# Depthwise convolution split between TensorE and VectorE: 13 taps as full diagonal matmuls against 16 taps as 32x32 diagonal blocks

## The chip, the cores and the metric

One core of a Trainium2 chip runs the whole program in one launch. The metric is device time in microseconds (us), the median of three runs. A profile of one execution goes with it; its times count from its first instruction.

## What is computed

The reference is a stack of four transformer layers on 256 positions of 1024 channels: a convolution mixer with a dense feed-forward layer, a windowed attention layer with a mixture of eight experts, and two hybrid attention layers. The change touches only the depthwise convolution of the first mixer:

```
u = a * sigmoid(gate)                                # 256 positions x 768 channels
u_pad = pad(u, 30 zero positions in front)
c[s, ch] = sum over tap 0..30 of dw_w[tap, ch] * u_pad[s + tap, ch] + dw_b[ch]
c = silu(layer_norm(c))                              # mean and variance over the 768 channels
m = memory_attention(q_mem, mem_k, mem_v)
h = h + concat(c, m) @ w_out
```

## The kernel before

Activations lie with channels on the 128 partitions and the 256 positions along the row. The 768 channels of the convolution are six blocks `t` of 128 channels; `U[t]` (line 1063) holds one block with 30 zeros in front, so a tap is a slice `U[t][:, tap:tap + 256]`. In TensorE terms the weights of a matmul are its stationary operand and the slice is its moving one.

`conv_layer` (line 1057) first projects the input: a loop over `c` = 0, 1, 2 makes two channel blocks at a time from a value half and a gate half, with weights that are split in two fp32r parts (ScalarE writes the high part, VectorE the low part) and three matmuls for each product. VectorE scales the result, ScalarE takes the sigmoid, VectorE writes `U[t]`. Then the 31 taps of a block are shared out. VectorE does the first 18: one `tensor_scalar` and 17 `scalar_tensor_tensor` into `cv[c]` (lines 1099 to 1104). TensorE does the last `PE_TAPS` = 13 in `taps(t)` (line 1067): for each tap ScalarE makes a 128x128 diagonal matrix from the identity (line 1076), and a full fp32 matmul multiplies it with the slice of `U[t]`, all into half of one PSUM bank. After two blocks one VectorE instruction adds that bank to `cv[c]` (line 1081). The profile shows an fp32 matmul as two records.

After the taps come the layer norm (lines 1128 to 1156: a mean by matmul with a constant matrix, subtraction, squares, variance, a reciprocal root on VectorE, a broadcast by matmul, silu, and the split in two fp32r parts), the queries and keys of the memory attention (`mem_first`, line 1017, has sixteen fp32 matmuls 512 columns wide), the memory attention itself, and the output projection `residual` (line 1044) into `xT`. Its first six of eight feed blocks come from the convolution, the last two from the attention. The feed-forward layer needs `xT`.

The order of the instructions is not that of the code. Every operation is recorded with its buffers (`Recorder`), and `issue` (line 555) plays the engines forward in time with prices from `cost` (line 391): each engine takes the first operation in order of priority that is ready and gets its buffers. Priority is the place in the code in TensorE time plus a bias in ns; a negative bias (`TAP_BIAS`, line 38, for the taps on both engines) pulls an operation forward. All operations are issued from line 699, so in the profile they share that line, and go by the kinds of their buffers: `large` (28 buffers for weights, also the diagonal matrices), `gen` (38 buffers for activations), `bank` (the 8 PSUM banks), `ct` and `pt` (constants and parameters). A PSUM bank that is held by one tile is free for another only when its last reader has run; so the eight banks are shared by the projections, the taps, `mem_first` and the layer norm. All DMAs are issued in order from SyncE's queue. `stream` (line 464) is the order's model of TensorE's clock.

Of the kernel before, what the change touches and what calls it, by code (L numbers as in the profile page):

```python
# [11 lines left out]
F32 = mybir.dt.float32  # L12
# [3 lines left out]
OP = mybir.AluOpType  # L16
# [20 lines left out]
PE_TAPS = 13  # L37
TAP_BIAS = -5e3
# [70 lines left out]

def _pairs_cols():  # L110
    return np.concatenate([np.arange(h * HD, (h + 1) * HD) for p in SWA_PAIRS for h in p])
# [5 lines left out]
def _params(i):  # L117
# [5 lines left out]
        ("dw_w", i["cv_dw_w"][0].reshape(CW, 6, 128).transpose(2, 1, 0).reshape(128, 6 * CW)),  # L123
# [25 lines left out]
def _consts():  # L149
# [26 lines left out]
    def add(n, a):  # L176
        nonlocal at
        a = np.ascontiguousarray(a, dtype=f)
        cols[n] = (at, a.shape[1])
        out.append(a)  # L180
        at += a.shape[1]

    add("ident", np.eye(128))
    add("ones", np.ones((128, 128)))
# [158 lines left out]
class Recorder:  # L343
# [47 lines left out]
    def cost(eng, name, outs, ins, kw):  # L391
# [8 lines left out]
        if eng == "PE":  # L400
            w = n(outs[0])
            if name == "transpose":
                w *= 2
            elif ins[0].dtype == F32R:
                w = max(256, w) * 16 / 15 + 4
            else:
                w = 4 * max(w, n(ins[0])) + 6
                if outs[0].ap[0][1] == 32:
                    w /= 4
            return (w + 6) / 2.4, 0.0  # L410
# [9 lines left out]
    def add(self, eng, name, fn, args, kw):  # L420
# [9 lines left out]
        op.work = (op.dur * 2.4, ins[0].ap[0][1] / 128) if eng == "PE" else None  # L430
# [271 lines left out]
class Net:  # L702
# [354 lines left out]
    def conv_layer(self):  # L1057
# [9 lines left out]
        def taps(t):  # L1067
            nc.bias = TAP_BIAS
            dt = [nc.tile("raw", [128, 8, 128]) for _ in range(2)]
            c = cv[t // 2][:, t % 2]  # L1070
            if t % 2 == 0:
                self.pd = self.mm("pcv")
            pd = self.pd[:, t % 2 * S:t % 2 * S + S]
            for n, tap in enumerate(range(CW - PE_TAPS, CW)):
                dg = dt[n // 8][:, n % 8]
                nc.scalar.activation(dg, self.C("ident"), AF.Copy, scale=self.P("dw_w", t * CW + tap))
                nc.tensor.matmul(pd, dg, U[t][:, tap:tap + S], start=n == 0 and t % 2 == 0,
                                 stop=n == PE_TAPS - 1, skip_group_check=True)
            if t % 2:
                c = cv[t // 2]  # L1080
                nc.vector.tensor_tensor(c, c, self.pd.rearrange("p (a s) -> p a s", a=2), op=OP.add)
            nc.bias = 0
# [623 lines left out]
```

## Time and profile before

| | |
|---|---|
| median of three runs | 2171.06 us (2170.19 to 2176.07) |
| the profiled execution | 2170.37 us, of which the profile's span is 2168.5 us |
| TensorE busy in the span | 2129.9 us, granted clock 0.993 of full speed |
| VectorE and ScalarE busy | 976.4 us and 739.3 us |
| the convolution layer | from 0 to about 130 us of the span |

TensorE is busy nearly throughout, so the question for any change is what its own work costs, and whether another engine makes it wait. A matmul's record also holds its latency, so a row's mean is longer than the pace at which matmuls follow one another: the pace is read from how many start in a stretch that is full.

### The profile page before, as it was taken

What the parts mean: (1) busy time and instruction counts of PE and PEld (TensorE: products, weight loads), DVE (VectorE), ACT (ScalarE), POOL (GpSimd) and SP (SyncE); (2) the same over time, 40 slices, a digit from 0 to 9 for tenths busy, and PEclk for the clock granted to TensorE, in tenths of its full rate; (3) what the DMA queues carried; (4) which work ended last, traced back from release to release, by engine and by line L of the source; (5) the groups of instructions that cost most, each with busy time, mean ns of one, the idle gap of its engine ahead of it and who ended that gap; (6) DMA issues with size and microseconds to landing.
All of it is one profiled execution on the core that took longest, in us unless ns stands there. A gap on an engine that the chain in (4) does not pass through costs nothing. (4 is left out here: it accounts for less than half of the span.)

```text
span 2168.5 us, 57713 instructions
## 1 busy us (share of the span) xinstructions
PE 2129.9 (98%) x25554; PEld 1684.8 (78%) x25554; DVE 976.4 (45%) x2085; ACT 739.3 (34%) x1318; POOL 0.2 (0%) x4
## 2 busy tenths in 40 slices
PE   8999999999999999999999999999999999999998
PEld 8799998766565566656565655788999998899997
DVE  8985569530211102020211120666675566667553
ACT  8574447510100001010101010645554454555442
POOL 0000000000000000000000000000000000000000
PEclk9999999999999999999999999999999999999998
DMA  7445554489999999999999997753456555345550
GB/s 260 158 146 191 176 191 159 163 306 407 379 345 406 373 407 342 384 384 405 368 364 378 401 374 285 256 191 113 154 190 194 183 182 188 113 137 194 194 183 29
DMA packets 155633, 555.70 MB, mean 256 GB/s; under 512 B 17392, under 2 KB 20080, under 8 KB 155376
## 3 DMA queue, kind: packets, MB, share of 16 engines
q1 hardware_dynamic: 155376, 551.94, 70.0%
q8 instruction: 202, 3.31, 0.6%
q14 instruction: 55, 0.45, 0.1%
HBM read 550.82 MB, written 1.05 MB: 254 GB/s over the span
## 5 line engine op out<-in xcount | busy, mean ns | idle before, releaser
L699 PE MATMUL bank<-large,gen 128*32 128x256 f32 (+2 forms) x16528 | 1049.3, 379 | 2.7 <-PEq L1330 2.7
L699 PE MATMUL bank<-gen,large 128*128 128x256 f32 x7488 | 934.8, 285 | 9.8 <-ACT large L699 8.1
L699 PEld LDWEIGHTS bank<-large,gen 128*32 128x32 f32 (+1 forms) x16528 | 648.8, 114 | 368.0 <-issue 11.0
L699 PEld LDWEIGHTS bank<-gen,large 128*128 128x128 f32 x7488 | 908.9, 189 | 25.9 <-issue 9.9
L699 DVE TENSOR_TENSOR large<-large,large 128x1024 fp32r<-128x1024 f32 (+1 forms) x364 | 438.5, 1210 | 134.1 <-PE bank L699 91.0
L699 ACT ACTIVATE large<-large 128x1024 fp32r<-128x1024 f32 (+1 forms) x364 | 373.5, 1045 | 241.6 <-PE bank L699 108.2
L699 ACT ACTIVATE gen<-bank 32x256 fp32r<-32x256 f32 (+6 forms) x315 | 121.2, 395 | 917.1 <-PE bank L699 905.8
L699 DVE SCALAR_TENSOR_TENSOR gen<-bank,small,gen 128x256 f32<-128x256 f32 (+2 forms) x100 | 44.3, 446 | 681.3 <-ACT gen L699 681.3
L699 ACT ACTIVATE gen<-gen 128x512 f32<-128x512 f32 (+3 forms) x145 | 86.9, 611 | 156.7 <-DVE gen L699 155.5
L699 DVE TENSOR_TENSOR gen<-bank,gen 32x256 fp32r<-32x256 f32 (+2 forms) x166 | 83.1, 508 | 125.3 <-PE bank L699 65.1
L699 PE MATMUL bank<-gen,gen 128*128 128x192 f32 (+5 forms) x668 | 108.7, 343 | 9.4 <-ACT gen L699 6.0
L699 DVE TENSOR_TENSOR gen<-gen,gen 128x512 f32<-128x512 f32 (+3 forms) x126 | 79.2, 636 | 53.0 <-ACT gen L699 51.3
L699 PEld LDWEIGHTS bank<-gen,gen 64*128 64x128 f32 (+3 forms) x668 | 67.8, 176 | 45.0 <-DVE gen L699 15.8
L699 PE MATMUL bank<-ct,gen 128*128 128x128 f32 (+2 forms) x366 | 62.8, 276 | 8.0 <-DVE gen L699 8.0
L699 PEld LDWEIGHTS bank<-ct,gen 128*128 128x128 f32 (+1 forms) x366 | 44.1, 156 | 24.4 <-issue 12.3
L699 DVE TENSOR_TENSOR xT<-xT,bank 128x512 f32<-128x512 f32 x64 | 43.5, 686 | 24.4 <-PE bank L699 23.5
L699 ACT ACTIVATE gen<-bank,small 128x256 f32<-128x256 f32 (+2 forms) x75 | 41.0, 569 | 31.1 <-PE bank L699 23.6
L699 DVE SCALAR_TENSOR_TENSOR gen<-bank,gen 128x256 f32<-128x256 f32 (+1 forms) x66 | 25.4, 428 | 54.7 <-PE bank L699 54.2
L699 DVE SCALAR_TENSOR_TENSOR gen<-gen,pt,gen 128x256 f32<-128x256 f32 (+1 forms) x120 | 49.0, 485 | 1.7 <-ACT gen L699 1.7
L699 ACT ACTIVATE gen<-gen,small 128x128 f32<-128x128 f32 x72 | 31.8, 443 | 17.8 <-DVE small L699 17.8
L699 PE MATMUL bank<-large,large 128*32 128x256 f32 (+1 forms) x416 | 37.6, 373 | 0.0
L699 DVE STREAM_TRANSPOSE gen<-gen 128x256 f32<-128x256 f32 (+1 forms) x90 | 36.0, 406 | 2.6
(62 smaller groups left out, 412.7 us busy)
## 6 DMA issues: line engine op xcount, KB each, us to landing
large<-e_in SPq DMA_DIRECT2D x448, 512.0 KB, 7.1
large<-e_down SPq DMA_DIRECT2D x224, 512.0 KB, 7.4
large<-c_up SPq DMA_DIRECT2D x64, 512.0 KB, 4.5
large<-c_dn SPq DMA_DIRECT2D x64, 512.0 KB, 4.7
large<-c_g SPq DMA_DIRECT2D x48, 512.0 KB, 3.8
large<-c_qk SPq DMA_DIRECT2D x24, 512.0 KB, 4.8
large<-cv_gate SPq DMA_DIRECT2D x22, 512.0 KB, 4.8
large<-cv_up SPq DMA_DIRECT2D x22, 512.0 KB, 5.6
```

What stands on the lines that cost most here:

```text
L699: op.fn(*[real(x) for x in op.args], **{k: real(x) for k, x in op.kw.items()})
```

## The change

`PE_TAPS` goes from 13 to 16, so VectorE keeps 15 taps of a block. The diagonal matrices of ScalarE go; a block's 16 diagonals are made as 32x32 diagonal blocks by one VectorE instruction, `dg` of 128 partitions x 16 x 32. A tap then is four matmuls of 32 rows by 32 columns, each on its own 32 rows of the array. So that sixteen such matmuls touch sixteen different places of the array, taps are dealt out by `_turn`: tap turn `n` puts its row group `r` on the output partitions of group `(r + n) % 4`. For that SyncE issues six DMAs for each block that write three copies of `U[t]` turned by 32, 64 and 96 partitions, and the four matmuls read the copy that fits; all 64 matmuls of a block wait for all six. The four turns add up in four PSUM banks, where one was used, and four VectorE adds bring them into `cv[c]`. The parameters of the taps are turned on the host in the same way. `TAP_BIAS` goes from -5e3 to -20e3, and the order's prices get an entry for a matmul of 32x32, a full fp32 matmul's divided by 5.2.

```diff
-PE_TAPS = 13
-TAP_BIAS = -5e3
+PE_TAPS = 16
+TAP_BIAS = -20e3
...
+def _turn(n):
+    return (n - CW + PE_TAPS) % 4 if n >= CW - PE_TAPS else 0
+
+
+def _turned(w):
+
+    return np.stack([np.roll(w[:, :, n], -32 * _turn(n), axis=0) for n in range(w.shape[2])], 2)
...
-        ("dw_w", i["cv_dw_w"][0].reshape(CW, 6, 128).transpose(2, 1, 0).reshape(128, 6 * CW)),
+        ("dw_w", _turned(i["cv_dw_w"][0].reshape(CW, 6, 128).transpose(2, 1, 0)).reshape(128, 6 * CW)),
...
+    add("ident4", np.tile(np.eye(32), (4, 1)))
...
                 if outs[0].ap[0][1] == 32:
-                    w /= 4
+                    w /= 4 if ins[0].ap[0][1] > 32 else 5.2
...
-        op.work = (op.dur * 2.4, ins[0].ap[0][1] / 128) if eng == "PE" else None
+        op.work = (op.dur * 2.4, max(32, ins[0].ap[0][1]) / 128) if eng == "PE" else None
+        if op.work and ins[0].ap[0][1] == 32:
+            op.work = op.dur * 2.4, 1
...
         def taps(t):
             nc.bias = TAP_BIAS
-            dt = [nc.tile("raw", [128, 8, 128]) for _ in range(2)]
-            c = cv[t // 2][:, t % 2]
+            turned = nc.tile("raw", [128, 3, CW - 1 + S])
+            moves = []
+            nc.bias = -2 * LOAD_FIRST
+            for n in range(1, 4):
+                at = 128 - 32 * n
+                nc.sync.dma_start(turned[:at, n - 1], U[t][32 * n:])
+                moves.append(nc.ops[-1])
+                nc.sync.dma_start(turned[at:, n - 1], U[t][:32 * n])
+                moves.append(nc.ops[-1])
+            nc.bias = TAP_BIAS
+            dg = []
+            all16 = [128, PE_TAPS, 32]
+            dg = self.t(all16, F32, "dg")
+            nc.vector.tensor_tensor(dg, self.C("ident4")[:, None, :].to_broadcast(all16),
+                                    self.P("dw_w", t * CW + CW - PE_TAPS, PE_TAPS)[:, :, None].to_broadcast(all16),
+                                    op=OP.mult)
             if t % 2 == 0:
-                self.pd = self.mm("pcv")
-            pd = self.pd[:, t % 2 * S:t % 2 * S + S]
-            for n, tap in enumerate(range(CW - PE_TAPS, CW)):
-                dg = dt[n // 8][:, n % 8]
-                nc.scalar.activation(dg, self.C("ident"), AF.Copy, scale=self.P("dw_w", t * CW + tap))
-                nc.tensor.matmul(pd, dg, U[t][:, tap:tap + S], start=n == 0 and t % 2 == 0,
-                                 stop=n == PE_TAPS - 1, skip_group_check=True)
+                self.pd = [self.mm("pcv") for _ in range(4)]
+            for tap in range(CW - PE_TAPS, CW):
+                n = _turn(tap)
+                for r in range(4):
+                    rows = slice(32 * r, 32 * r + 32)
+                    j = 32 * ((r + n) % 4)
+                    x = turned[rows, n - 1, tap:tap + S] if n else U[t][rows, tap:tap + S]
+                    nc.tensor.matmul(self.pd[n][j:j + 32, t % 2 * S:t % 2 * S + S], dg[rows, tap - CW + PE_TAPS], x,
+                                     start=tap < CW - PE_TAPS + 4 and t % 2 == 0, stop=tap >= CW - 4, skip_group_check=True)
+                    nc.ops[-1].deps.update(moves)
             if t % 2:
                 c = cv[t // 2]
-                nc.vector.tensor_tensor(c, c, self.pd.rearrange("p (a s) -> p a s", a=2), op=OP.add)
+                for p in self.pd:
+                    nc.vector.tensor_tensor(c, c, p.rearrange("p (a s) -> p a s", a=2), op=OP.add)
             nc.bias = 0
```

## Rows read from the trace of the kernel before

**Rows 1.** The page's busy times of the engines, share of the span, instructions.

```profile
PE 2129.9 (98%) x25554; PEld 1684.8 (78%) x25554; DVE 976.4 (45%) x2085; ACT 739.3 (34%) x1318; POOL 0.2 (0%) x4
```

**Rows 2.** Stretches: start:end, length, busy us (instructions) by engine, clock, DMA share, GB/s.

```profile
29.00:45.00 16.00, 16.00 (x128) 15.73 (x126) 13.47 (x33) 15.97 (x45) 0.00 (x0) 1.00 0.65 220
45.00:62.00 17.00, 17.00 (x92) 15.27 (x92) 17.00 (x43) 10.78 (x36) 0.00 (x0) 1.00 0.28 93
62.00:79.50 17.50, 17.50 (x82) 15.32 (x82) 17.50 (x44) 6.59 (x8) 0.00 (x0) 1.00 0.35 113
79.50:106.00 26.50, 26.50 (x125) 18.11 (x124) 24.94 (x79) 14.66 (x22) 0.00 (x0) 0.94 0.60 195
106.00:131.00 25.00, 23.89 (x173) 19.69 (x172) 16.07 (x66) 18.10 (x47) 0.00 (x0) 1.00 0.13 47
```

**Rows 3.** TensorE by shape, 58 to 78 us: count, busy us, mean ns, idle before.

```profile
L699 PE MATMUL bank<-gen,large 128*128 128x256 f32 x94 | 20.5, 378 | 0.0
```

**Rows 4.** VectorE and ScalarE by shape, 0 to 260 us: same columns.

```profile
L699 DVE SCALAR_TENSOR_TENSOR gen<-gen,pt,gen 128x256 f32<-128x256 f32 x108 | 43.3, 486 | 1.7 <-ACT gen L699 1.7
L699 DVE TENSOR_TENSOR gen<-gen,gen 128x512 f32<-128x512 f32 x25 | 16.9, 690 | 4.2 <-ACT gen L699 3.5
L699 DVE TENSOR_TENSOR gen<-gen,bank 128x512 f32<-128x512 f32 x3 | 2.0, 690 | 0.0
L699 ACT ACTIVATE large<-ct,pt 128x128 f32<-128x128 f32 x78 | 23.8, 387 | 0.0
```

**Rows 5.** VectorE in order of time: start, length, what, count [idle before <- releaser].

```profile
29.84 1.89 DVE L699 TENSOR_TENSOR gen<-bank,gen 128x512 f32<-128x512 f32 x3 [1.42 <-ACT gen L699]
33.42 0.89 DVE L699 SCALAR_TENSOR_TENSOR gen<-gen,pt,gen 128x256 f32<-128x256 f32 x2 [1.69 <-ACT gen L699]
34.22 0.73 DVE L699 TENSOR_SCALAR gen<-gen,pt 128x256 f32<-128x256 f32 x2
34.87 13.55 DVE L699 SCALAR_TENSOR_TENSOR gen<-gen,pt,gen 128x256 f32<-128x256 f32 x34
...
81.73 1.29 DVE L699 TENSOR_TENSOR gen<-gen,bank 128x512 f32<-128x512 f32 x2
```

**Rows 6.** ScalarE in order of time, just before the first sigmoid.

```profile
29.71 1.85 ACT L699 ACTIVATE large<-ct,pt 128x128 f32<-128x128 f32 x6
31.58 1.28 ACT L699 ACT_TABLE_LOAD   x1
32.88 0.91 ACT L699 ACTIVATE gen<-gen,pt 128x256 f32<-128x256 f32 x2
```

**Rows 7.** Experts, 750 to 800 us, as in rows 2: matmuls of 32 columns.

```profile
750.00:800.00 50.00, 50.00 (x932) 30.16 (x928) 4.18 (x12) 1.98 (x6) 0.00 (x0) 1.00 1.03 408
```

**Rows 8.** TensorE in order of time: layer norm's matmuls, then the attention's scores.

```profile
83.29 1.46 PE L699 MATMUL bank<-gen,ct 128*128 128x256 f32 x6
84.40 3.23 PE L699 MATMUL bank<-large,gen 128*128 128x256 f32 x24
87.46 0.59 PE L699 MATMUL bank<-gen,ct 128*128 128x256 f32 x2
...
101.80 0.60 PE L699 MATMUL bank<-gen,ct 128*128 128x256 f32 x2
...
116.58 2.00 PE L699 MATMUL bank<-gen,gen 64*128 64x256 f32 x16
...
122.83 0.30 PE L699 MATMUL bank<-ct,gen 128*128 128x128 f32 x1 [1.11 <-DVE gen L699]
```

**Rows 9.** VectorE and ScalarE inside the layer norm, in order of time.

```profile
88.09 0.38 ACT L699 ACTIVATE gen<-bank 128x256 f32<-128x256 f32 x1 [15.74 <-PE bank L699]
...
98.93 0.48 DVE L699 TENSOR_SCALAR gen<-ct,small 128x128 f32<-128x128 f32 x2
```

**Rows 10.** The page's DMA issues: count, KB each, median us to landing.

```profile
outT<-xT SPq DMA_DIRECT2D x4, 256.0 KB, 2.2
gen<-alibi SPq DMA_DIRECT2D x12, 192.0 KB, 4.6
```

## The prediction, made before the change was run

> **What bounds the kernel now.** I read the page's busy times first: TensorE works in 2129.9 of 2168.5 us [rows 1], so time is won by less TensorE work, unless the stretch in question waits for something else. The stretch in question is the convolution layer, so I looked at its parts next [rows 2]. There TensorE is full from 29 to 106 us, and VectorE is full from 45 to 79.5 us and nearly so on either side. Two engines are full at once: what TensorE saves is won only as far as VectorE's chain lets the layer end sooner. ScalarE is full only before 45 us; later it has room. The DMA share is 0.28 to 0.35 while the taps run.
>
> What TensorE does there follows from counts. From 58 to 78 us it starts 94 records in 20 us, 213 ns each [rows 3]. An fp32 matmul leaves two records: the eight score matmuls of the attention (four heads, two blocks of positions) leave 16 [rows 8]. So a tap costs 2 x 213 = 427 ns, and the 78 taps 33.3 us. From 45 to 79.5 us 174 records start [rows 2], and 156 belong to taps: TensorE does nearly nothing but taps there, beside VectorE's taps. Then VectorE's order: it starts on `U[0]` at 33.4 us, does taps almost without a gap until the last adds at 81.73 to 83.0 us [rows 5], and the layer norm comes after. Inside the layer norm VectorE and ScalarE wait for TensorE, which is in the middle of other work: the mean's last matmul starts at 87.46 us though `cv` was whole at 83.0 [rows 5, 8], and the broadcast, ready at 99.4, starts at 101.8 [rows 8, 9]. TensorE's first gap after the start is 1.11 us at 122.8 [rows 8]. By 131 us the feed-forward layer runs.
>
> **The change, part by part.**
>
> *TensorE's taps* go from 78 matmuls to 16 x 6 x 4 = 384, or 768 records. No row shows a matmul of 32 rows by 32 columns. The nearest is the experts' stage, where four matmuls of 128 rows by 32 columns stand side by side in one bank: 932 records in 50 us, 53.6 ns each [rows 7], a quarter of 213. That row says four column groups work at once. The scores say the same of two row groups: 16 records of 64 rows in 2.00 us, 118 ns or less, where one after the other they would take 3.4 us [rows 8]. So the bounds are 53.6 ns (only the columns count: 768 x 53.6 = 41.2 us) and 213 / 16 = 13.3 ns (all sixteen places at once: 10.2 us). What issuing a weight load and a matmul costs keeps the upper part of this span likelier, since no row has a pace under 53.6 ns. I take about 41 ns, 31.5 us, between the nearest row and some help from the row groups; the planner's own price (a full matmul's divided by 5.2) says 32.6 us, but that is a number in the code. Against 33.3 us that saves 1.8 us; the ends are 7.9 us more and 23.1 us less.
>
> The Trainium skill (TensorE: Matmul & The Clock Gate, Part 3: Packing small matmuls) measured sixteen 32x32 tiles at 10.6 times the speed of one after another, with two-byte data. By that ratio 384 x 427 ns = 164 us would become an estimated 15.5 us. No row here has such a matmul; the experts' row bears out a factor of four only.
>
> *VectorE* loses 3 x 6 = 18 `scalar_tensor_tensor`. Thirty-four of them take 13.55 us in a row, 0.40 each [rows 5], so 7.2 us go. It gains nine more adds out of a bank: two follow one another in 1.29 us, so 0.60 each and 0.69 alone [rows 4, 5], 5.4 us. And it gains six `dg` products of 512 elements, for which the nearest row is the 128x512 product at 0.60 to 0.69 us [rows 4], 3.6 to 4.1 us. They depend on constants only, so the two holes at 28.4 and 31.7 us (1.42 and 1.69 us [rows 5]) and the time before cover them; without that cover they are on VectorE's chain. Sum on the chain: 1.8 us less with the cover, 2.3 us more without it. I take 1 us less.
>
> *ScalarE* loses 78 diagonals, 23.8 us [rows 4]. Nearly all of that lies beside other work. One piece is on the path: six diagonals run from 29.71 to 31.56 us, only then the table for the sigmoid is loaded (1.28 us), and VectorE waits 1.69 us for the sigmoid [rows 5, 6]. Without them the table is loaded during VectorE's products (29.84 to 31.7), the sigmoid starts about 1.1 us sooner, and so does VectorE's chain.
>
> *SyncE and the copies.* 36 DMAs of 36 to 110 KB, 2.6 MB in all, in a stretch with two thirds of the DMA time free [rows 2]. They wait for `U[t]` on an in-order queue, behind which the loads for later stand; these are needed tens of us later. A copy is there some 2.2 us (the store of `xT`) to 4.6 us (`alibi`) after its issue [rows 10], so block `t` can start that much after `U[t]`. For the last two blocks, `U` at some 66 us, the taps start near 70 and need 10.5 us: before VectorE's own taps end. I count nothing, at most 3 us.
>
> *Changes of tile shape.* Six blocks of 64 matmuls stand between full-size ones. A record lasts 378 ns where the next starts after 213 [rows 3], so if the array empties at a change of shape, one costs up to 0.17 us: 12 changes, at most 2 us. I take 1.
>
> *PSUM banks.* Each pair of blocks now holds four banks of eight, and gives them back after VectorE's adds. The two projections ahead hold four more at some 37 us, so the second pair's banks come free only when VectorE has done the first adds, which its taps outrank. TensorE has `mem_first` to do meanwhile (in the run before it comes after the taps), but that takes two banks too. The last pair's second half can then start only after the second pair's adds, at 79 to 81 us, and ends some 5 us later plus two adds: `cv` whole at 83 to 89 us instead of 83.0. I count half a microsecond in the forecast; a larger size is a rival.
>
> *The sum*, against the profiled execution's 2170.4 us: TensorE -1.8, the start of the chain -1.1, VectorE -1, of which the path takes the smallest common part, since both engines must fit: about -2. Shape changes +1, banks +0.5, and some -1.5 because `mem_first` has moved ahead of the layer norm and no longer stands in front of its matmuls (the two waits above are 4.5 and 2.4 us). That is 2168.4. The median lies 0.7 us above the profiled run: 2169 us. The rest of the kernel keeps its work; a new order of it may move it by 2 us either way.
>
> **The rivals.**
>
> *Better packing.* At 13 to 25 ns a record the taps take 10 to 19 us, and TensorE has 14 to 23 us too many. Then VectorE's chain sets the end: 1.8 less work, 1.1 earlier start, and both waits in the layer norm gone (4.5 + 2.4, less about 1.5 that the matmuls take): 8 us less, 2162 or so. TensorE would show gaps between 70 and 100 us. For it: row groups do run side by side [rows 8]. Against it: no row below 53.6 ns.
>
> *Only the columns count (slower).* At 53.6 ns the taps cost 7.9 us more on an engine that has no gap from 29 to 106 us; with the 1 us for shape changes and 1.5 us won elsewhere it is 2178. It decides from about 49 ns on, where the taps cost 4.5 us more. A fall of the clock in these stretches (it shows 0.94 from 79.5 to 106 us, 1.00 in all other parts [rows 2]) would act alike.
>
> *Banks.* `cv` whole 6 us later, partly made good in the layer norm: +3 to +8, about 2176.
>
> *One place of a bank at a time.* If the four row groups of a tap took turns because they write one bank, the 768 records would follow at 213 ns, 164 us, and the kernel at some 2300. The trace shows only column groups sharing a bank [rows 7]; the two row groups of the scores write two banks. The Trainium skill (TensorEngine Tiling, Gotcha 1: PSUM Pressure) says that different row tiles can't access one PSUM bank at the same time; no run here shows whether partitions of their own lift that.
>
> **How the numbers follow.** A measurement of this kernel can tell about 0.3% (6.5 us) from no change, so "same" is 2164.5 to 2177.6. Forecast 0.48 (0.05 faster, 0.40 same, 0.03 slower), better packing 0.25 (0.20 faster, 0.05 same), columns only 0.14 (0.03 same, 0.11 slower), banks 0.08 (half same, half slower), turns 0.05 (slower). Faster 0.25, same 0.52, slower 0.23. The range leaves out the turns and the far ends: 2160 to 2180.
>
> **What would show it.** The pace of the 32x32 records in a full stretch: 41 ns for the forecast, under 25 for the first rival, 53.6 for the second, 213 for the last. VectorE's last add near 82 us and no diagonals on ScalarE; the first `U` about 1 us sooner. Gaps on TensorE between 70 and 100 us speak for better packing, waits of TensorE for VectorE's adds for the banks. I would be wrong first of all in the pace, for which no row exists, and next in the banks.

## The result and the profile after

The changed kernel takes 2193.76 us (2189.04 to 2196.0) against 2172.79 us (2170.19 to 2178.51) of the kernel before, measured side by side: a ratio of 1.009, interval 1.0078 to 1.0103. It is 21 us slower, where 2169 us and at most 2180 us were forecast. The profiled execution of the changed kernel took 2191.66 us, its span is 2189.9 us. One execution of e7, of 5458 us, is left out of the ratios that follow.

The busy times of the engines on the page after, which answer to [rows 1]:

```profile
PE 2138.6 (98%) x26166; PEld 1675.7 (77%) x26166; DVE 980.1 (45%) x2082; ACT 716.2 (33%) x1240; POOL 0.2 (0%) x4
```

ScalarE lost 23 us of work, VectorE's work hardly moved, and TensorE is busy for 8.7 us more, though its taps were to become shorter. The stretches of [rows 2] in the kernel after, and the next one (same columns):

```profile
29.00:45.00 16.00, 15.08 (x244) 12.94 (x243) 16.00 (x43) 5.17 (x11) 0.00 (x0) 1.00 0.26 62
45.00:62.00 17.00, 12.32 (x215) 8.08 (x215) 14.81 (x36) 2.92 (x4) 0.00 (x0) 0.85 0.40 112
62.00:79.50 17.50, 17.50 (x47) 6.21 (x46) 3.60 (x8) 0.00 (x0) 0.00 (x0) 0.50 0.17 59
79.50:106.00 26.50, 24.62 (x471) 19.35 (x469) 23.11 (x47) 4.11 (x6) 0.00 (x0) 0.91 0.61 203
106.00:131.00 25.00, 22.79 (x76) 13.96 (x75) 19.50 (x75) 18.65 (x32) 0.00 (x0) 0.80 0.77 272
131.00:156.00 25.00, 23.89 (x180) 20.16 (x179) 16.46 (x59) 14.81 (x37) 0.00 (x0) 1.00 0.13 46
```

The third line holds the answer. From 62 to 79.5 us TensorE counts as busy throughout, yet starts 47 records in 17.5 us, at a granted clock of 0.50 (1.2 GHz of 2.4), and VectorE stands still for all but 3.6 us. Before, VectorE was full there [rows 2]. What TensorE does in that stretch, in order of time:

```profile
61.03 1.06 PE L711 MATMUL bank<-gen,gen 32*32 32x256 f32 x2
62.02 0.58 PE L711 MATMUL bank<-gen,large 128*128 128x256 f32 x1
62.53 1.06 PE L711 MATMUL bank<-gen,gen 32*32 32x256 f32 x4
63.53 0.58 PE L711 MATMUL bank<-gen,large 128*128 128x256 f32 x1
```

Two to four records of 32x32 alternate with one single full-size record, the projection of the third pair of blocks, and one such alternation takes 1.50 us (61.03 to 62.53). From 60 to 81 us the tile shape changes 26 times, in the whole kernel 32 times between 32x32 and larger. An alternation with four small records takes no longer than one with two (62.53 to 63.53 us against 61.03 to 62.02). So the projection that VectorE needs creeps, and VectorE waits for it:

```profile
80.66 0.69 DVE L711 TENSOR_TENSOR gen<-bank,gen 128x512 f32<-128x512 f32 x1 [15.06 <-PE bank L711]
...
100.64 0.68 DVE L711 TENSOR_TENSOR gen<-gen,bank 128x512 f32<-128x512 f32 x1
```

The second line is the last add of a bank: the convolution is whole at 101.3 us, before at 83.0 us [rows 5]. The order allowed this because priority is the place in the code plus the bias: a bias of -20e3 puts the taps of a block among the projections of the third pair instead of ahead of them or behind.

Where the small matmuls stand in one piece they are fast. Two stretches inside such pieces (same columns as [rows 2]):

```profile
40.00:42.00 2.00, 1.86 (x93) 1.05 (x77) 2.00 (x7) 0.00 (x0) 0.00 (x0) 1.00 0.52 133
54.00:56.00 2.00, 2.00 (x72) 1.27 (x64) 2.00 (x6) 0.00 (x0) 0.00 (x0) 1.00 0.41 92
```

That is 21.5 and 27.8 ns a record, about 25. Two blocks of the experiments that run without a gap, in e10 and in e1, bound it: 128 records in 2.47 and in 4.08 us, 19 and 32 ns. What sets the pace between the two is not settled.

```profile
79.80:82.30 2.50, 2.47 (x128) 1.82 (x128) 2.50 (x4) 1.50 (x2) 0.00 (x0) 1.00 0.02 7
64.90:69.00 4.10, 4.08 (x128) 2.76 (x128) 4.10 (x8) 0.91 (x2) 0.00 (x0) 1.00 0.14 56
```

SyncE's queue changed as well. Its DMA issues (start, time from the first to the end of the last, what, count), first after, then before:

```profile
35.08 7.80 SPq L711 DMA_DIRECT2D large<-gen  x12
42.98 2.27 SPq L711 DMA_DIRECT2D large<-cv_qm  x2
51.74 8.83 SPq L711 DMA_DIRECT2D large<-gen  x12
60.67 1.02 SPq L711 DMA_DIRECT2D large<-w_mkv  x2
83.60 7.75 SPq L711 DMA_DIRECT2D large<-gen  x12
...
94.25 2.23 SPq L711 DMA_DIRECT2D large<-cv_out  x4
```

```profile
31.88 3.63 SPq L699 DMA_DIRECT2D large<-w_mkv  x4
37.70 25.71 SPq L699 DMA_DIRECT2D large<-cv_out  x5
```

A copy (`large<-gen`) costs SyncE 0.65 us to issue (7.80 / 12), and each dozen waits for its `U[t]`. Behind them the weights of the output projection, `cv_out`, are issued from 94 us on instead of 37.7, and the memory's weights `w_mkv` at 60.7 to 94 instead of 31.9 to 35.5.

Where the first pair starts, the answer to [rows 5], VectorE in order of time:

```profile
29.72 0.68 DVE L711 TENSOR_TENSOR gen<-ct,pt 128x512 f32<-128x512 f32 x1
...
32.17 1.88 DVE L711 TENSOR_TENSOR gen<-bank,gen 128x512 f32<-128x512 f32 x3
...
34.57 0.88 DVE L711 SCALAR_TENSOR_TENSOR gen<-gen,pt,gen 128x256 f32<-128x256 f32 x2
```

The first line is the last of four products `dg` in front of the pair. The pair's own products start at 32.17 us (before 29.84) and its `U` at 34.57 us (before 33.42).

**A balance of the layer.** TensorE shows what each kernel lost. Two rows of each kernel suffice: the stretch from 30 to 160 us, and the first 512-wide matmul of the second layer, up to which all kernels have done the same work but for the taps (2254 other matmul records, in e5 four more). Before, then after:

```profile
30.00:160.00 130.00, 128.89 (x832) 112.10 (x831) 117.20 (x310) 87.52 (x183) 0.00 (x0) 0.99 0.47 158
```

```profile
30.00:160.00 130.00, 119.19 (x1251) 83.71 (x1250) 96.44 (x267) 48.64 (x91) 0.00 (x0) 0.86 0.43 139
```

```profile
327.76 6.13 PE L699 MATMUL bank<-large,gen 128*128 128x512 f32 x26
```

```profile
350.03 5.26 PE L711 MATMUL bank<-large,gen 128*128 128x512 f32 x22
```

At that mark the kernel after is 22.3 us late, and 1839.9 us of its span are left, as against 1840.7: all of the loss lies in the first layer. TensorE's idle time grew by 9.7 us (10.81 against 1.11), and the clock took the equivalent of 16.9 us (0.13 less over 130 us; two digits, so within 0.7 us). The experiments supply the two other terms, the pace of the taps and the price of a change of shape; the sum stands behind them.

### The profile page after: what moved, and what is told of

It reads as the page before. It is cut to its first block, busy times and chain, and to the rows that moved or that the text cites. A ratio compares the mean times of both kernels' runs of the same rounds, so it can differ in the third digit from the quotient of the medians.

```text
span 2189.9 us, 58885 instructions
## 1 busy us (share of the span) xinstructions
PE 2138.6 (98%) x26166; PEld 1675.7 (77%) x26166; DVE 980.1 (45%) x2082; ACT 716.2 (33%) x1240; POOL 0.2 (0%) x4
## 5 line engine op out<-in xcount | busy, mean ns | idle before, releaser
L711 PE MATMUL bank<-large,gen 128*32 128x256 f32 (+3 forms) x17104 | 1083.6, 382 | 10.5 <-DMA large<-gen 5.5
L711 PEld LDWEIGHTS bank<-large,gen 128*32 128x32 f32 (+2 forms) x17104 | 667.3, 114 | 385.6 <-issue 15.7
L711 PE MATMUL bank<-gen,large 128*128 128x256 f32 x7332 | 905.5, 283 | 10.6 <-ACT large L711 7.7
L711 PEld LDWEIGHTS bank<-gen,large 128*128 128x128 f32 x7332 | 879.2, 189 | 33.9 <-issue 21.8
L711 PE MATMUL bank<-gen,gen 32*32 32x256 f32 (+6 forms) x860 | 127.8, 361 | 10.3 <-ACT gen L711 7.5
L711 PEld LDWEIGHTS bank<-gen,gen 64*128 64x128 f32 (+4 forms) x860 | 73.0, 159 | 47.1 <-DVE gen L711 15.4
L711 PE MATMUL bank<-ct,gen 128*128 128x128 f32 (+2 forms) x366 | 63.7, 278 | 10.8 <-DVE gen L711 7.5
L711 DVE SCALAR_TENSOR_TENSOR gen<-gen,pt,gen 128x256 f32<-128x256 f32 (+1 forms) x102 | 41.8, 477 | 1.8 <-ACT gen L711 1.8
```

The source lines that it names most:

```text
L711: op.fn(*[real(x) for x in op.args], **{k: real(x) for k, x in op.kw.items()})
```

## The experiments

In all of them `dma_start(turned ...)` are the copies, and `prio` is the place in the order (smaller is earlier).

**e1, the small matmuls of a block in one piece.**

```diff
                     nc.ops[-1].deps.update(moves)
+                    nc.ops[-1].prio, nc.ops[-1].load = -1e6 + 1e4 * t + 1e-2 * tap + 1e-3 * r, 0.0
```

> The changed kernel with one thing altered: the 64 tap matmuls of a channel block get one priority each block that outranks all else on TensorE, so that they stand together. The order has 8 changes between 32x32 and full-size matmuls where the changed kernel has 32, of which 26 fall between 60 and 81 us. Theory A (single 32x32 matmuls between single full ones cost some 0.75 us a change, with TensorE's clock at 0.5): about 17 us go, 2174 to 2178 us, and VectorE's wait of 15 us for the third pair of projections goes with them. Rival B (the four banks, their adds and the copies hold the layer up): the time stays at 2188 to 2194 us and the wait only changes its name.

Measured: 2176.24 us (2174.6 to 2181.1), ratio 1.0032 (1.0019 to 1.0044). There are 8 changes of shape in place of 32. The third and the fourth stretch of [rows 2] in e1:

```profile
62.00:79.50 17.50, 15.13 (x361) 11.62 (x359) 17.50 (x42) 0.91 (x2) 0.00 (x0) 1.00 0.45 126
79.50:106.00 26.50, 24.37 (x154) 15.82 (x155) 21.78 (x71) 13.58 (x20) 0.00 (x0) 0.81 0.97 356
```

From 62 to 79.5 us VectorE is full again and the clock 1.00. So 13 us (by the ratios, 0.0058 of 2172) to 17 us (by the medians) of the 21 are the alternation and what hung on it; at the mark of the balance it is 16.7. What is left: TensorE starts the last pair's second half only after VectorE's adds of the second pair,

```profile
81.63 5.22 PE L711 MATMUL bank<-large,gen 32*32 32x256 f32 x68 [2.40 <-DVE gen L711]
```

and the convolution is whole at 88.15 us. In all, TensorE waits from 30 to 160 us mostly for copies (`DMA large<-gen`) and for VectorE (waited for: us in total, times, longest):

```profile
PE bank L711 <- DMA large<-gen: 6.4, 4, 2.8
PE bank L711 <- DVE gen L711: 2.9, 2, 2.4
```

After 79.5 us the DMA share is 0.97, where it was 0.60 [rows 2]: the loads kept back by the copies now come all at once.

**e2 and e3, the bias alone.** e2 is the kernel after with the bias of the kernel before, e3 the kernel before with the bias of the kernel after:

```diff
-TAP_BIAS = -20e3
+TAP_BIAS = -5e3
```

> The changed kernel with TAP_BIAS at the -5e3 of the kernel before. The order then has 88 changes of shape. Theory A: 56 changes more at about 0.75 us, so 2225 to 2235 us. Rival B (the number of changes doesn't matter, only that the taps come too early or hold banks): no more than 2195 us, since the projections are no longer outranked.

> The kernel before with TAP_BIAS at -20e3: the same order rule, all tap matmuls full-size. Theory A (the shape, not the order, is what costs): 2168 to 2176 us, clock near 1.00 from 40 to 80 us. Rival C (pulling the taps ahead of the projections costs by itself): 2182 us or more, with VectorE waiting for the projections.

Measured, in one execution each: e2 2227.07 us, e3 2173.59 us, against 2169.94 us of the kernel before. e2 changes shape 88 times. Its trace shows the price of a change at both clocks, because the clock falls in the middle of the alternation:

```profile
45.15 0.61 PE L711 MATMUL bank<-large,gen 32*32 32x256 f32 x2
45.70 0.38 PE L711 MATMUL bank<-gen,large 128*128 128x256 f32 x1
46.01 0.61 PE L711 MATMUL bank<-large,gen 32*32 32x256 f32 x2
...
49.86 1.06 PE L711 MATMUL bank<-large,gen 32*32 32x256 f32 x4
50.86 0.58 PE L711 MATMUL bank<-gen,large 128*128 128x256 f32 x1
51.37 1.06 PE L711 MATMUL bank<-large,gen 32*32 32x256 f32 x2
```

From 45.15 to 46.01 us an alternation takes 0.86 us, from 49.86 to 51.37 us 1.51 us. The first pace belongs to a granted clock of 0.99 (40 to 47 us), the second to one of 0.50 (50 to 90 us). The work in it is one full record of a projection, 0.12 us (a run of 154 takes 18.44 us, under e16), and two to four small ones at 25 ns: so beside its work at the pace of full stretches an alternation costs, for each of its two changes of shape, (0.86 - 0.20) / 2 = 0.33 us at full clock and (1.51 - 0.40) / 2, about 0.55 us, at half. Not all of that is the change. A small matmul that stands alone has nothing beside it to share the time with: four matmuls side by side, eight records, take 8 x 54.8 ns = 0.44 us in e4 below, and in the kernel after two take as long as one (the lines from 61.03 us). If a lone one takes that long too, 0.86 - 0.12 - 0.44 = 0.30 us are left for two changes, an estimate of 0.15 us each. The Trainium skill (TensorEngine Tiling (Array Packing), Key Properties) says that a change of tiling mode drains TensorE; these 0.15 us agree with that, though no run here looks inside. e3 has the same bias with full-size taps, and its stretch keeps the clock and its length:

```profile
62.00:79.50 17.50, 17.50 (x92) 15.57 (x92) 16.89 (x39) 4.70 (x6) 0.00 (x0) 1.00 0.46 151
```

So it is not the bias and not the order as such, but the order together with two tile shapes.

**e4, no copies: each tap on four places of the array.** The four row groups write straight down into one bank, and no turned copies exist; the order is that of e1.

```diff
-    return (n - CW + PE_TAPS) % 4 if n >= CW - PE_TAPS else 0
+    return 0
...
-            turned = nc.tile("raw", [128, 3, CW - 1 + S])
-                nc.sync.dma_start(turned[...], ...)
...
-                self.pd = [self.mm("pcv") for _ in range(4)]
+                self.pd = [self.mm("pcv")]
```

> The blocks of the first kernel of this set, without the turned copies: the four matmuls of a tap always use the four places on the array's diagonal, one bank and one add for a pair of blocks, no DMA. If the pace comes from the number of places in use: four places, 53 ns a record, 41 us for all taps (with sixteen places the changed kernel shows 18 to 25 ns in a full stretch), and about 2172 to 2182 us. If the pace is set by issue alone: 18 to 25 ns a record here too, and faster than the kernel before, about 2162 to 2168 us, since neither copies nor nine adds are needed.

Measured: 2179.11 us (2174.39 to 2183.15), ratio 1.0036 (1.0024 to 1.0048).

```profile
38.30 14.02 PE L711 MATMUL bank<-gen,gen 32*32 32x256 f32 x256
```

256 records in 14.0 us are 54.8 ns each, with no gap and the clock at 1.00. With sixteen places it was 25 ns. So the number of places in use sets the pace (e4 also writes one bank where four were written; that the bank holds it back is unlikely, as projections write a bank of their own every 0.12 us, but no run parts the two), and four places cost what the experts' four column groups cost, 53.6 ns [rows 7]. With no copies and one add for a pair, TensorE idles no more than before (1.06 us from 30 to 160 us), and the kernel is late by the longer taps: 768 x 54.8 = 42.1 us against 33.3.

**e5 and e6, the loads ahead of the copies.** e5 is e1 with all taps placed behind the memory's loads in the code; e6 pulls the adds of the banks forward as well.

```diff
-EARLY = 6
+EARLY = 0
```

```diff
                     nc.vector.tensor_tensor(c, c, p.rearrange("p (a s) -> p a s", a=2), op=OP.add)
+                    nc.ops[-1].prio, nc.ops[-1].load = -1e6 + t, 0.0
```

> The blocks of e1 with EARLY at 0: the taps are recorded after the query and mem_first, so that the loads of their weights come ahead of the copies on SyncE (in e1 the four loads of w_mkv go out at 60.7 to 79.0 us, behind the copies of U; before, at 31.9 to 35.1). Theory D (in e1 TensorE's saved time turns into some 10 us of idling between 45 and 85 us because the work it could do has no weights yet, and that work then stands in front of the layer norm as it did before): idle falls under 4 us, the 512-wide matmuls come before the mean, 2164 to 2171 us. Rival E (VectorE's chain alone sets the end): w_mkv comes early and the time stays at 2174 to 2178.

> e5, and the adds out of the four banks outrank VectorE's taps, so that banks come free as soon as a pair's matmuls are done. If TensorE's wait for banks (2.9 us at 81.6 us in e1, where the last pair's second half starts only after the second pair's adds) is on the path: 2 to 4 us less than e5. If not: the same as e5 within 1.5 us.

Measured: e5 2188.14 us, ratio 1.0069 (1.0045 to 1.0092); e6 2184.83 us, ratio 1.0057 (1.004 to 1.0075). Both are slower than e1, so as tried this was no cure, and the 3 us between them lie inside their intervals. `w_mkv` now comes at 20 us, but in e6 the 36 copies stand in SyncE's queue in one row from 37.3 to 79.5 us and `cv_out` still comes after them, at 79.6 to 93.5 us.

**e7 and e8, more taps on TensorE.** e6 with 20 and 24 taps there, 11 and 7 on VectorE (`dg` then is made in two parts).

```diff
-PE_TAPS = 16
+PE_TAPS = 20
```

> e6 with 20 taps on TensorE and 11 on VectorE: 24 scalar_tensor_tensor of 0.40 us fewer (9.6 us), 192 records at 25 ns more (4.8 us). If VectorE's chain sets the end of the convolution layer in e6: some 6 to 9 us less than e6. If TensorE does: some 4 us more than e6.

> e6 with 24 taps on TensorE and 7 on VectorE: 48 scalar_tensor_tensor fewer (19.2 us), 384 records at 25 ns more (9.6 us), so about 29 us of tap matmuls on TensorE against 33.3 us in the kernel before. If VectorE's chain still sets the end: some 12 us less than e6, under 2160 us. If TensorE has become the bound: about the time of e7.

Measured: e7 2175.92 us, ratio 1.0014 (1.0004 to 1.0024); e8 2177.65 us, ratio 1.0027 (1.0016 to 1.0037). Four taps fewer on each of six blocks win 9 us over e6, four more win nothing. VectorE's taps then no longer set the end: the last add of a bank ends at 98.0 us in e7 and at 103.2 us in e8, though VectorE has fewer taps there.

**e9 and e10, the copies moved to another queue.** e9 is e1 with the adds of e6, and with the products `dg` made to wait for the first pair's second `U`. e10 has one change more:

```diff
-                nc.sync.dma_start(turned[...], ...)
+                nc.scalar.dma_start(turned[...], ...)
```

> Like e1 (the small matmuls of a row tile in one block on TensorE), and two orders on VectorE mended besides: the add of a pair's banks goes ahead of the remaining taps, and the product that makes the diagonal blocks waits until the second row tile of the first pair is there, so that it stands no longer ahead of the first pair. The copies stay on SyncE. Theory F (what is left over before the change is the loads of cv_qm, w_mkv and cv_out standing behind 36 copies in SyncE's queue): the wait of TensorE for a bank, 2.9 us in e1, goes, but the weights of cv_out are still issued behind the copies, from about 79 us, and ScalarE's copies of them stand ahead of the layer norm; 2173 to 2177. Rival G (VectorE is what is left: its later start and the wait for the banks): the first row tile is whole about 1.5 us sooner than in e1 and the time falls by 3 to 4 us, to 2172.

> The kernel of e9 with one thing moved: the 36 copies are issued from ScalarE's queue and not from SyncE's, so that no load stands behind a copy in a queue. Theory F: cv_qm, w_mkv and cv_out are issued as in the kernel before (cv_out from some 40 us on), ScalarE has made their high parts before the mean of the layer norm, the clock stays at 1.00 there, and the time falls to 2164 to 2170, 5 us or more under e9. Rival H (the loads are held by the pool of buffers in which the turned copies lie, not by the queue): cv_out is issued late as in e9, and the time is that of e9 within 2 us; then ScalarE's 0.65 us for each issue shows as well, by a later sigmoid of the second pair, 2176 to 2180.

Measured: e9 2183.98 us (2181.67 to 2187.94), ratio 1.0057 (1.0044 to 1.007); e10 2176.75 us (2172.94 to 2181.36), ratio 1.0026 (1.0016 to 1.0036). e9 was to be faster than e1 and is 5 us (by the ratios) to 8 us (by the medians) slower: 24 copies now stand in a row on SyncE's queue, and `cv_qm`, which TensorE could fill its gaps with, is issued at 58.0 us (43.8 in e1). SyncE in e9, then in e10:

```profile
33.95 23.98 SPq L711 DMA_DIRECT2D large<-gen  x24
58.03 1.04 SPq L711 DMA_DIRECT2D large<-cv_qm  x2
...
78.15 13.16 SPq L711 DMA_DIRECT2D large<-cv_out  x8
```

```profile
20.73 2.46 SPq L711 DMA_DIRECT2D large<-cv_qm  x2
...
39.68 46.72 SPq L711 DMA_DIRECT2D large<-cv_out  x8
```

With the copies gone from that queue the loads go out as before, and 7.2 us are won: the queue was a cost of its own, by the one edit that differs. The pool of buffers, the rival, did not hold them. But the time is not under 2170 us as the theory had it. VectorE in e10, fully busy from 40 to 100 us, makes low parts of weights (`large<-large,large`) between its last taps and adds:

```profile
87.56 0.67 DVE L711 TENSOR_TENSOR gen<-gen,bank 128x512 f32<-128x512 f32 x1
88.23 1.21 DVE L711 TENSOR_TENSOR large<-large,large 128x1024 fp32r<-128x1024 f32 x1
89.37 0.67 DVE L711 TENSOR_TENSOR gen<-gen,bank 128x512 f32<-128x512 f32 x1
```

and the mean's last matmuls come at 93.70 us.

**e11, e10 with 20 taps on TensorE** and three blocks' taps ahead of the query (`PE_TAPS = 20`, `EARLY = 3`).

> The kernel of e10 with 20 taps on TensorE and 11 on VectorE, and only three of the six row tiles' taps placed ahead of the query and the memory weights. 192 small matmuls more at 25 ns are 4.8 us on TensorE, 24 taps fewer on VectorE at 0.4 us are 9.6 us. Theory F: with the loads in time VectorE is again what ends last ahead of the layer norm, so fewer taps there bring 4 to 9 us over e10: 2158 to 2165. Rival I (TensorE's own work fills the stretch whatever VectorE does, as e7 and e8 showed with the copies on SyncE): 2172 to 2177, and TensorE idle less than 3 us between 30 and 110 us.

Measured: 2181.59 us, ratio 1.0043 (1.0028 to 1.0058). Slower than e10; the gain of 4 to 9 us did not come, and the rival's 2172 to 2177 us were missed too. Why it is slower is not settled.

**e12, the one constant.** The kernel after with the bias doubled, nothing else:

```diff
-TAP_BIAS = -20e3
+TAP_BIAS = -40e3
```

> The kernel after with one constant changed: the shift of the taps in the planned order is twice as large (40e3 in place of 20e3), so that small matmuls no longer fall between the projections of the third pair; 6 changes of shape in place of 32. The theory that the alternation and the halved clock make the 17 us between after and e1: 2174 to 2180, with the wait of VectorE for the third pair gone and the clock above 0.9 from 60 to 80 us. The rival that e1 won by the order within a block and not by the block: above 2185.

Measured: 2178.31 us (2175.79 to 2181.75), ratio 1.0034 (1.0024 to 1.0044). There are 6 changes of shape, the clock is 1.00 from 60 to 80 us, and VectorE's wait for the third pair is gone. As e1, by another way: the alternation was the cause.

**e13 to e15, low parts later.** e13 is e10 with the low parts of `cv_out` made only after the last add; e14 and e15 have 18 and 20 taps on TensorE besides, and `EARLY = 4`.

```diff
             nc.vector.tensor_tensor(lo, raw, hi, op=OP.subtract)
+            nc.ops[-1].deps.update(self.hold)   # the last add, for cv_out
```

> The kernel of e10 with one wait more: the low parts of the weights of cv_out are made by VectorE only after the last add of the banks. Theory J (VectorE's order sets the layer norm): in e10 eight low parts of 1.2 us stand between 80 and 93 us ahead of the last add; about six of them go behind it, the mean's matmuls start at 86 to 88 us in place of 93.7, and the time falls by 3 to 6 us against e10, to 2171 to 2174. Rival K (what is left lies behind the attention): the mean comes sooner, but the low parts are then late for the output projection or stand in the layer norm's own work, and the time stays within 2 us of e10, 2175 to 2179.

> The kernel of e13 with 18 taps on TensorE and 13 on VectorE, and four of the six row tiles' taps placed ahead of the query and the memory weights. VectorE is rid of 12 taps at 0.40 us, 4.8 us, and has six products of 128x64 more, about 0.2 us each; TensorE has 96 small matmuls more, 2.4 us at 25 ns. Theory J: the mean's matmuls start 3 us sooner than in e13 and the time is 2167 to 2172. Rival K: no gain over e13, 2174 to 2179.

> The same with 20 taps on TensorE and 11 on VectorE: 24 taps fewer than in e13 on VectorE, 9.6 us, less six products of 128x128 at about 0.25 us. Theory J: the mean's matmuls start 6 to 8 us sooner than in e13, at about 80 us, ahead of the 83.3 us of the kernel before, and the time is 2163 to 2169. Rival K: 2174 to 2179, as e11, which had as few taps on VectorE.

Measured: e13 2176.53 us, ratio 1.0021 (1.0012 to 1.0031); e14 2185.99 us, 1.0063 (1.0049 to 1.0077); e15 2173.22 us, 1.0008 (0.9999 to 1.0017). e14 misses both of its ranges and is 9 us slower than e13, which no run here explains. In e13 the convolution is whole at 88.8 us and the mean's last matmuls start at 90.74, 3 us sooner than in e10, for the same time: that order was worth nothing. In e15 the adds end at 80.8 us, sooner than before, but TensorE then does 512-wide memory matmuls, and the mean is late:

```profile
85.20 7.11 PE L711 MATMUL bank<-large,gen 128*128 128x512 f32 x16
...
97.75 1.03 PE L711 MATMUL bank<-gen,ct 128*128 128x256 f32 x4
```

**e16 to e18, the layer norm first.** e15, e13 and the kernel before, each with the layer norm, from the mean to the split of its result, pulled forward.

```diff
+        nc.bias = -40e3
         pm = self.mm("pm")[:, :S]
...
+        nc.bias = 0
         if LATE:
```

> The kernel of e15 (20 taps on TensorE, copies from ScalarE's queue, low parts later) with the layer norm of the convolution, from the mean to the split of its result, pulled 40e3 ns forward in the planned order, so that the 512-wide memory matmuls no longer stand between the last add of the banks and the mean. Theory L (this order eats the gain of the shorter work): the mean's last matmul starts at 82 to 85 us in place of 97.75, the convolution's result is ready some 10 us sooner, TensorE has the memory matmuls to fill the layer norm's waits, and the time falls by 4 to 9 us against e15, to 2164 to 2169. Rival M (the memory attention ends last and not the layer norm, so the memory matmuls put later cost what the norm wins): within 2 us of e15 or slower, 2172 to 2178.

> The same move in the kernel of e13 (16 taps on TensorE). There the 512-wide matmuls before the mean were already done in part ahead of the last block, and the mean's last matmul started at 90.74 us, 2.6 us after the last add. Theory L: about 2 us to win, 2172 to 2176. Rival M: 2175 to 2179.

> The kernel before with the same move of the layer norm and nothing else. There VectorE's adds end at 83.0 us and the mean's last matmul starts at 87.46 us. If the gain belongs to the order and not to the small matmuls, this one gains as well: 4 us at the mean and 2 us at the broadcast, 2165 to 2169. If TensorE, which has no gap there, only changes the order of the same work, the time stays within 2 us of the kernel before, 2170 to 2174.

Measured: e16 2171.69 us (2168.57 to 2175.56), ratio 0.9999 (0.999 to 1.0007); e17 2177.52 us, 1.0028 (1.0019 to 1.0037); e18 2171.76 us, 0.9992 (0.9983 to 1.0002). In e16 the mean's last matmuls start at 81.32 us, 6 us sooner than in the kernel before [rows 8], and the long run of projections behind the attention at 126.75 us, before at 130.10:

```profile
81.32 1.03 PE L711 MATMUL bank<-gen,ct 128*128 128x256 f32 x4
...
126.75 18.44 PE L711 MATMUL bank<-gen,large 128*128 128x256 f32 x154
```

Yet the first 512-wide matmul of the second layer starts at 327.67 us, before at 327.76 us. Against e15 the move brings that mark forward by 6.4 us in the profiled executions (334.12 us in e15), but the medians differ by 1.5 us only and their intervals overlap; e17 wins nothing over e13, and e18 nothing over the kernel before. So an earlier layer norm by itself is worth little or nothing, as TensorE must do the same work up to that mark.

**The balance of the runs.** The taps cost 33.3 us before; at 25 ns 768 records cost 19.2 us, 14.1 less. A change of shape is counted at 0.33 us; between blocks, where the small records keep their pace, that is up to 0.18 us too much for each. Idle and clock are the differences to the kernel before in the row from 30 to 160 us, the last column the difference at the first 512-wide matmul of the second layer, all in us:

| kernel | taps | changes of shape | clock | idle | sum | measured at the mark |
|---|---|---|---|---|---|---|
| after | -14.1 | 32: +10.6 | +16.9 | +9.7 | +23.1 | +22.3 |
| e1 | -14.1 | 8: +2.6 | +5.2 | +9.4 | +3.1 | +5.6 |
| e4 (54.8 ns) | +8.8 | 6: +2.0 | 0 | 0 | +10.8 | +9.9 |
| e9 | -14.1 | 6: +2.0 | +7.8 | +18.7 | +14.4 | +12.9 |
| e10 | -14.1 | 6: +2.0 | +2.6 | +15.4 | +5.9 | +4.5 |
| e12 | -14.1 | 6: +2.0 | +3.9 | +15.2 | +7.0 | +7.2 |
| e13 | -14.1 | 6: +2.0 | +5.2 | +12.1 | +5.2 | +2.6 |
| e16 (20 taps) | -9.3 | 2: +0.7 | +2.6 | +8.5 | +2.5 | -0.1 |

It closes within 3 us in these eight. Of the runs that the table leaves out, worked in the same way, e3, e5, e11, e14, e17 and e18 close within 3 us as well; e2, e6, e7, e8 and e15 come out 3 to 7 us too high (e7 +16.2 against +9.3, e15 +11.9 against +6.4). One reason is that time at the lower clock in which TensorE idles is counted twice: in e6 TensorE is at work for 9.39 of the 17 us from 104.6 to 121.6 us, all at 0.50. So the balance says where the time went, not to a microsecond.

With sixteen places TensorE did save on the taps, 14 us where it does 16 of them. In every arrangement this came back as idle time, because blocks of small matmuls wait for VectorE's `U`, for copies and for banks where the long taps had filled the time (the waits under e1), and in most of them as time at the lower clock. That gaps bring the clock down is not shown: e4 has neither, but e17 has 13.7 us more idle time than the kernel before and the same clock:

```profile
30.00:160.00 130.00, 115.18 (x1433) 94.77 (x1434) 116.19 (x302) 64.38 (x113) 0.00 (x0) 0.99 0.53 171
```

**What stays open.** e10 and e13 have medians 4.6 us above the kernel before, though the profiled execution of e13 has a span of 2168.6 us, as the kernel before; it was its fastest (2170.41 us of 2170 to 2180), so for e13 the balance explains the best case only. Its executions differ in the granted clock over the whole span, 0.993 in the two fastest and 0.990 to 0.991 in the three slowest, and 0.003 of 2170 us is 6.5 of the 10 us; why the clock differs is not settled. No variant was found that is faster than the kernel before; e16 and e15 equal it.

## Why the prediction was wrong

**The step that failed is "Changes of tile shape".** It counted 12 changes at up to 0.17 us, 1 us in the sum. There were 32, 26 of them between 60 and 81 us, at 0.33 us each by what an alternation takes at full clock, and the alternation ran at half clock: +10.6 us and, of the clock's 16.9 us, what e1 lacks of them, 11.7. For the change alone its price was near (an estimate of 0.15 us by e2 and e4); what it had wrong is their number, that a small matmul alone between full ones gets nothing of the packing, and the clock. The step took for granted that "six blocks of 64 matmuls stand between full-size ones", in one piece. The diff said otherwise: priority is the place in the code plus a bias, and a bias of -20e3 had to be set against the places of the third pair's projections. No rival had this mechanism (the rival of the columns names a fall of the clock, without a cause or a price), and so the range ended at 2180.

**The pace** was the declared weak spot, and was wrong the other way: about 25 ns (19 to 32), not 41. The bounds of 13.3 and 53.6 ns hold it. The choice near the upper end rested on "no row has a pace under 53.6 ns"; e4 shows why none had one, since that is what four places cost (54.8 ns), and sixteen cost half of it. By the Trainium skill's ratio (TensorE: Matmul & The Clock Gate, Part 3: Packing small matmuls), 10.6, a record would take 213 / 10.6 = 20 ns, an estimate; the traces show 19 to 32 ns, so the ratio here is 7 to 11, and that page was the better guide of the two. Its table is for 512 columns and names no data type; the taps are fp32 with 256.

**Better packing, the rival,** was right on the pace and on the gaps of TensorE, and wrong on its 2162 us. It took gaps on TensorE to be free, with VectorE's chain as the end. With changes of shape mended (e1, e10, e13) the gaps are there, 9 to 15 us of them, and no gain: VectorE's chain was not shorter (the convolution is whole at 88 to 94 us), and what TensorE missed in the gaps it had to do later. In e16, with 20 taps on TensorE, VectorE's adds do end sooner than before, at 80.5 us, and there is no gain either: 8.5 us of idle time and 2.6 us of the clock take up the 9.3 us that its taps save.

**SyncE and the copies,** counted as "nothing, at most 3 us", cost 7.2 us where they could be separated (e9 against e10). The sentence "needed tens of us later" was wrong for `cv_qm` and `w_mkv`, with which TensorE fills its time, and for `cv_out`, which the queue put off by 57 us. The landing of a copy was right: 2.2 us on the page after for the 107 KB ones. Its cost is the issue, 0.65 us each on an in-order queue, and the wait for `U` at the queue's head.

**VectorE's early start** had the wrong sign. `U` came 1.15 us later (34.57 against 33.42), not 1.1 us sooner. The diagonals did leave ScalarE, but the table load comes at 31.99 us (before 31.58 [rows 6]), because the freed engines took up the memory's squares and scales, and four `dg` products and the memory's sums stand before the pair's products on VectorE. The holes that were to cover `dg` were not where `dg` ran.

**Banks** had the right mechanism: in e1 TensorE waits 2.4 us for the adds of the second pair and the convolution is whole at 88.15 us, inside the 83 to 89 us of that step; half a microsecond was too little. In the kernel after it is hidden behind the alternation.

**The layer norm's waits** were to lose 1.5 us because `mem_first` had moved ahead. In the kernel after it lies behind the mean instead, its weights being late; and e16 and e18 show that such a move is worth nothing at the end.

**One reading** was a little off: at 213 ns for a record of a tap and 0.12 us for one of a projection, the 174 records from 45 to 79.5 us hold some 146 of taps, not 156. No term of the sum rests on it.

**Right** were the 2 us for the rest of the kernel (1839.9 against 1840.7 us behind the mark; in the variants 1835 to 1845), VectorE's work (980.1 against 976.4 us), and that the four row groups of a tap don't take turns at one bank: 213 ns a record appeared in no block of small matmuls, and e4, where all of a block's four groups write one bank, runs at 54.8 ns. The Trainium skill's rule (TensorEngine Tiling (Array Packing), Gotcha 1: PSUM Pressure) does not bind here, where each group has its own partitions of the bank.

## What to carry to other kernels

Before small tiled matmuls are priced, write out the order in which they meet full-size ones, and count changes of shape: here a small matmul alone between full ones cost 0.66 us more than its records in a block, and the alternation cost the clock too. When two engines are full side by side, work taken off one of them is won only as far as it does not come back there as gaps; here it came back even where the other's chain got shorter as well (e16). A DMA put on an in-order queue is priced by what stands behind it and by the wait at its head, not by its landing.

## What the runs showed of the hardware

- 32x32 fp32 records of 256 columns follow each other at 54.8 ns with four places of the array in use, and at 19 to 32 ns with sixteen. A full-size record takes 213 ns in the taps [rows 3] and 0.12 us in the projections (154 in 18.44 us, e16).
- Where one or two 32x32 matmuls alternate with single full-size records, each change of shape costs about 0.33 us at full clock and 0.55 us at half, the lost packing included; the change alone is some 0.15 us at full clock, an estimate (e2, e4). When single records of the two shapes alternate, the granted clock falls to 0.50 and stays there: from 62 to 79.5 us in the kernel after, from 50 to 90 us in e2, in both after some us of alternation at full clock (e2) or after blocks with gaps and single changes (after). With the same bias and full-size taps (e3) it stays at 1.00 from 29 to 79.5 us.
- A copy inside the core's memory of 36 to 107 KB lands 1.9 to 2.2 us after its issue from SyncE, 2.5 to 2.9 us from ScalarE's queue (e10), and takes SyncE 0.65 us.
